# Moving six state updates of the first scan group, and starting two sets of weight sums in the pooling stage

## The chip, the cores and the metric

The kernel runs on one core of one Trainium2 chip. A core has a matrix engine (PE, with PEld for its weight loads), a vector engine (DVE), a scalar engine (ACT), GpSimd (POOL), and SyncE (SP), which here only issues transfers. POOL computes next to nothing in this kernel: it issues transfers too, those that add into memory among them. Each engine works through its own list of instructions in the order in which the program placed them; an instruction waits on semaphores for what it reads and for the buffer that it overwrites. All transfers share 16 DMA engines. The metric is the device time of one execution in microseconds (us).

## The reference

One decoder layer over 528 positions (16 learned ones ahead of 512) of width 1024, in float32. Cut to what matters here:

```python
u = rmsnorm(h, mix_norm_w);  proj = u @ w_in            # pool, z, x/B/C, dt, gates
y_pool = (pool_mixer(proj[pool]) * pool_scale) @ w_pool_up
# pool_mixer: causal means over 2, 4, 8, 16 positions minus the input, then 256x256 per group
xbc = silu(causal_depthwise_conv(proj[xBC], conv_w, conv_b))     # 4 taps
# scan: 8 groups of 4 heads, chunks of 128 positions
cb     = einsum("bclgn,bcsgn->bclsg", c, b)
y_diag = einsum("bclsg,bclsgr,bcsgrp->bclgrp", cb, exp(a_cs_l - a_cs_s) * mask, xdt)
states = einsum("bclgn,bclgr,bclgrp->bcgrpn", b, decay, xdt)
h_next = chunk_decay * h + state                        # over the chunks
y_off  = einsum("bclgn,bcgrpn,bclgr->bclgrp", c, h_prev, exp(a_cs))
y_ssd  = (rmsnorm_groups((y_diag + y_off + d_skip * x) * silu(z)) * norm_w) @ w_ssd_out
h = h + (gate_pool * y_pool + gate_ssd * y_ssd) @ w_o
v = rmsnorm(h, mlp_norm_w);  hid = relu(v @ w_ff1);  h = h + (hid * hid) @ w_ff2
out = rmsnorm(h, final_norm_w)[:, 16:]
```

## The kernel before

**Products.** Every float32 factor is split into a rounded part and a rest (`whi`, `wlo` for weights; `uh`, `ul` for the normed input), and a product is three matmuls: high by high, low by high, high by low. A weight block (128 x 1024, 512 KB) comes by an SP transfer into one of three `raw` buffers, ACT casts `whi` out of it (line 111 or 132) and DVE subtracts to get `wlo` (line 113 or 133). Many large products are made in Strassen's manner, from sums of blocks with one product less. Sums of weight blocks needed for that are made ahead by POOL transfers, from DRAM to DRAM, some of which add: `weight_steps` issues eight for a set of `f1` and four for a set of `f2`, into tensors that the profile calls `f_t` and `f_s`. An adding transfer waits until the copy below it has landed. SP loads the finished sums much later, as `t`, `s` or `rawf`.

**Stages.** Start and the projections of group 0, to about 75 us; the scan of groups 0 to 7, each woven with the projections and convolutions of the next group, to about 455; the pooling stage, to about 553; the merge of both branches under the gates; the output projection `wo`; then the two layers of the MLP, which run into each other from about 672 on.

**The scan step.** `ssd` takes a group through these steps: it masks and decays the chunk products (`abc`, line 679, "masked" in the code), updates the state over the chunks (`st`, a multiplication on line 675 and an addition on line 676 for each of three chunks), multiplies the states by C (`po`, line 688) and the masked products by x (`py`, line 694), and sums both in `yt`. Meanwhile the projections of the next group go through PE into PSUM (`px`) and through a convolution of one first tap and three further taps on DVE (line 442) into `bt`, `ct` and `xc`. Wide PSUM tiles come from two buffers, so the third `px` tile can only begin when DVE has read the last tap out of the first.

**The pooling stage.** `pool_pair` forms four products of one pool group out of two weight blocks a1 and a2 (`raw_block`, SP's line 126): `whiA`/`wloA` from a1, then `sm` (lines 985 and 987) and two more sums, `whiS`, `whiD`, `whiB` and their rests. The projected input `pu` is averaged by DVE (`pw`, line 962), split into `ph` and `pl` (lines 973 and 974) and multiplied by the group's matrix (`pg`, `pool_mix`). POOL loads the kept accumulators (`acc`) and gates (`m`, line 1090) meanwhile.

**After the merge.** POOL loads the residual `ht` in four parts (line 1202) as soon as the buffers of the normed input are free, and then issues what is left of the sets, because the loop behind it runs `while sets`. In the MLP, ACT applies relu (1391) and the square (1392), DVE makes the sums of Strassen's left factors (`r`, lines 1518 to 1521, and `vs`, lines 1440 to 1443) and their rests (1449, 1513, 1523), and adds finished products from PSUM (`alpha`) to `ht` or takes them away (line 1240). A product on PE that needs alpha's PSUM again waits for that line.

**What sets the order.** The program is written in the order of the stages, and a scheduler places the instructions on the engines by priority: `tc.high_priority(n)` gives an instruction a place n instructions sooner, `tc.issue_after(x)` puts it behind x in the order.

Of the kernel before, what the change touches and what calls it, by code (L numbers as in the profile page):

```python
# [12 lines left out]
ALU = mybir.AluOpType  # L13
# [39 lines left out]

SETS_AT = {0: 1, 1: 1, 2: 2, 3: 1, 4: 2, 5: 2, 6: 1, 7: 1}
PIECES = {4: 21, 7: 14}
SETS_POOL = 0

PLAIN = 4

# [5 lines left out]
def kernel(ctx: ExitStack, tc, xT, x, w, fx, f1, f2, vec, fnw, out):  # L65
    nc = tc.nc
    act, dve, pe, pool = nc.scalar, nc.vector, nc.tensor, nc.gpsimd
# [47 lines left out]
    def block(behind=None, cast_behind=None):  # L115
        t = block_tiles()
        with tc.high_priority(100):
            block_load(t, slice(0, 1024))
            block_split(t, slice(0, 1024), behind, cast_behind)
        return t[2:]  # L120
# [51 lines left out]
    cdec = const.tile([P, 4, HEADS], F32, name="cdec")  # L172
# [17 lines left out]
    gate_d = [dram.tile([P, SEQ], F32, name=f"gate_d{d}") for d in range(NK)]  # L190
# [157 lines left out]
    for t, name in ((rsh, "dgh"), (rsl, "dgl")):  # L348
        d = pre.tile([NT, 6, NT], F32R, tag="sq", name=name, bufs=2)
# [3 lines left out]
    for i in range(2):  # L353
        pb = psum1(f"pb1_{i}")
        c = slice(3 * i, 3 * i + 3)
# [235 lines left out]
    def bc(ap, n):  # L591
        return ap.unsqueeze(len(ap.shape)).to_broadcast(list(ap.shape) + [n])

    def ssd(g, cur):

        xc, bt, ct, zt = cur
        hs = slice(R * g, R * g + R)
        tok = lambda c: slice(NM + c * P, NM + (c + 1) * P)
        ctok = lambda c: slice(c * P, (c + 1) * P)
        flat = lambda t: t.rearrange("p r d -> p (r d)")  # L600
# [45 lines left out]
        def decay():  # L646
            act.activation(abc[:, :2], abc[:, :2], AF.Exp, scale=-1.0)
            return act.activation(abc[:, 2:], abc[:, 2:], AF.Exp)
# [14 lines left out]
        st = [gs.tile([P, R, 64], F32, tag=f"st{c}", name=f"st{c}_{g}") for c in range(4)]  # L663
        pss = [psum1(f"pst{g}_{b}") for b in range(2)]
        pv = [pss[c // 2][:, (c % 2) * 256 : (c % 2) * 256 + 256] for c in range(4)]
# [5 lines left out]
        if g == G - 1:  # L671
            with tc.issue_after(st0.ins):
                decay()
        for c in range(3):
            dve.tensor_tensor(st[c + 1], st[c], bc(cdec[:, c, hs], 64), op=ALU.mult)
            last_state[g] = dve.tensor_tensor(flat(st[c + 1]), flat(st[c + 1]), pv[c + 1], op=ALU.add)
        for rs_ in ((slice(0, 2), slice(2, R)) if g == G - 1 else (slice(0, R),)):
            n = rs_.stop - rs_.start
            masked[g] = dve.tensor_tensor(dm[:, rs_], dm[:, rs_], cbm.unsqueeze(1).to_broadcast([P, n, 4, P]),
                                          op=ALU.mult)  # L680
        mark[0] = st[3][:, 0, :1]
        yield

# [45 lines left out]
    late_cast, last_state = [None], {}  # L729
    done, abc_load, masked, y_first, squared, b_meta, x_decayed = {}, {}, {}, {}, {}, {}, {}  # L730
# [17 lines left out]
    m1 = {}  # L748
# [23 lines left out]
    def weight_steps():  # L772
        t = sets.pop(0)
        src = {"fx": fx, "f1": f1, "f2": f2}[t[0]][t[1]]
        o = {n: wsum[(*t, n)] for n in SUMS[t[0]]}
        put = nc.gpsimd.dma_start
        yield put(o["t1"], src[B11])
        yield put(o["s3"], src[B12])
        yield put(o["t1"], src[B12], accum_op=ALU.add)
        if "t2" in o:  # L780
            yield put(o["t2"], src[B22])
        yield put(o["s3"], src[B22], accum_op=ALU.add)
        if "t2" in o:
            yield put(o["t2"], o["t1"], accum_op=ALU.add)
            yield put(o["t4"], src[B21])
            yield put(o["t4"], o["t2"], accum_op=ALU.add)

    def weight_sums():
        for end in weight_steps():
            pass  # L790
        return end
# [142 lines left out]
    for g in range(G):  # L934
        nxt = group_tiles(g + 1) if g + 1 < G else None
        fill = [group_proj(g + 1, nxt, GATE_AT.get(g))] if nxt else [out_part()]
        if g == 4:
            fill = [out_half()] + fill
        weave(ssd(g, cur), fill, 2 if g == 4 else 1, weight_sums_at(SETS_AT[g], PIECES.get(g, 12)),
              [sums_of_u(g)] if g in SUMS_AT else [])  # L940
        cur = nxt
# [26 lines left out]
    def pooled_halves(t, s, copied=None):  # L968
        ph = gp.tile([P, SEQ], F32R, tag="ph", name=f"ph{t}", bufs=3)
        pl_ = gp.tile([P, SEQ], F32R, tag="pl", name=f"pl{t}", bufs=3)  # L970

        with tc.issue_after(copied.ins) if copied is not None else nullcontext():
            act.copy(ph, s[:, NM:])
        dve.tensor_tensor(pl_, s[:, NM:], ph.bitcast(F32), op=ALU.subtract)
        return ph, pl_
# [57 lines left out]
    def pool_mix(gi, pooled, wgb):  # L1033
        ps = [psum1(f"pg{gi}_{j}") for j in range(2)]
        wh, wl = wgb
        for j in range(2):
            os = [(gi % 2) * 512 + k * 256 + j * P for k in range(2)]
            mm3s(ps[j], [((wh[:, o : o + P], wl[:, o : o + P]), pooled[k]) for k, o in enumerate(os)])
        for j in range(2):
            t = 2 * gi + j  # L1040
            h = yp.tile([P, SEQ], F32R, tag="yh", name=f"yph{t}")
            l = yp.tile([P, SEQ], F32R, tag="yl", name=f"ypl{t}")
            mixed[:] = [act.activation(h, ps[j], AF.Copy, scale=col(V_PS, t)),
                        dve.scalar_tensor_tensor(l, ps[j], col(V_PS, t), h.bitcast(F32),
                                                 op0=ALU.mult, op1=ALU.subtract)]
            yps[t] = (h, l)

    def gate_ssd(d):
        ps = psum1(f"pgs{d}")
        proj(narrow(ps), block(), U)  # L1050
        gt = gtp.tile([P, SEQ], F32, tag="gt", name=f"gs{d}")
        act.activation(gt, ps, AF.Sigmoid, bias=col(V_BG, NK + d))
        return gt

    for d in range(NK):
        t_load = nc.gpsimd.dma_start(acc[d], acc_d[d])
    for _ in range(SETS_POOL):
        with tc.issue_after(t_load.ins):
            t_load = weight_sums()
    pend = [pooled_halves(*a) for a in pool_pair(POOL_ORDER[0])]  # L1060

    un = units()
# [11 lines left out]
    for n in range(1, 4):  # L1074
        pend, ahead = nxt, None
        if n < 3:
            nxt, ahead = pool_pair(POOL_ORDER[n + 1]), POOL_ORDER[n + 1]
        if n == 2:
            wgb = block()
        else:  # L1080
            gts.append(gate_ssd(MERGE[len(gts)]))

        pend = [pooled_halves(*a, copied.get(ahead)) for a in pend]
        with tc.issue_after(last[ahead].ins) if n < 3 else nullcontext():
            pool_mix(POOL_ORDER[n], pend, wgb)
        if n == 1:
            for d in MERGE:
                with tc.issue_after(mixed[0].ins):
                    if d < NK - 1:
                        nc.gpsimd.dma_start(m1[d], gate_d[d])  # L1090
    pool_stack.close()
    tf_stack.close()
    wo_stack = ExitStack()
# [548 lines left out]
    c = NC - 1  # L1642
# [14 lines left out]
    for t in range(4):  # L1657
        T, st = t // 2, slice((t % 2) * P, (t % 2 + 1) * P)
# [187 lines left out]
```

## Time and profile before

| | |
|---|---|
| median of 3 runs | 1000.0 us (999.92 to 1001.16) |
| profiled execution | 1001.71 us |
| span of its trace | 1000.0 us |
| PE busy | 987.8 us, 99% of the span |
| DVE busy | 803.9 us |
| ACT busy | 602.2 us |
| granted PE clock | 0.998 |
| POOL transfers | 67.51 MB, 26.4% of 16 DMA engines' span |
| SP transfers | 109.00 MB, 32.7% |

The span is 1.7 us shorter than the execution's time; what lies outside it is start and end. PE is idle for 12.2 us of the span. A row of a timeline has the start, the duration, the engine and line, the tiles written and read, the number of instructions merged, and in brackets the idle time ahead with what ended it. A DVE instruction's successor starts a little before its own written end, so the cost of one in a row is read from start to start.

### The profile page before, as it was taken

Reading aid. Unit: us, or ns where it says so; the run is one execution under the profiler, and the core shown is the slowest. Engines: PE = TensorE matmul, PEld = TensorE weight load, DVE = VectorE, ACT = ScalarE, POOL = GpSimd, SP = SyncE. Lnnn points to the kernel's source line nnn. Section 1 sums busy time; section 2 is a strip of 40 time slices with the busy share of each in tenths; the row PEclk is TensorE's granted clock in tenths of the full one; section 3 lists DMA queues with packets and bytes.
Section 4 is the critical chain, followed back from the end, with each engine's and each line's share of the span. In section 5 each row is a group of like instructions: output and inputs, shape, how many; then the busy total and the mean of one; then the engine's idle time right before and its main releaser. Section 6 shows DMA issues by size and latency. Waiting matters only on the chain.

```text
span 1000.0 us, 15672 instructions
## 1 busy us (share of the span) xinstructions
PE 987.8 (99%) x6035; PEld 873.8 (87%) x6035; DVE 803.9 (80%) x1162; ACT 602.2 (60%) x855; POOL 119.5 (12%) x215
## 2 busy tenths in 40 slices
PE   9999999999999999999999999999999999999997
PEld 7889998989889999978898888888789999999986
DVE  7978997879845888988789666975988888888885
ACT  7657839495924658574345433477666656656654
POOL 0011321211212212223200001121000000000000
PEclk9999999999999999999999999999999999999999
DMA  7284968666798848768723723899354454454332
GB/s 261 78 254 149 268 197 214 190 191 212 230 271 235 245 129 259 226 163 171 271 85 127 253 85 112 228 243 314 92 190 148 148 190 144 152 186 150 129 106 85
DMA packets 61803, 184.52 MB, mean 185 GB/s; under 512 B 7072, under 2 KB 8416, under 8 KB 60704
## 3 DMA queue, kind: packets, MB, share of 16 engines
q1 hardware_dynamic: 39456, 109.00, 32.7%
q0 software_dynamic: 18240, 67.51, 26.4%
q10 hardware_dynamic: 4032, 7.00, 1.9%
q8 instruction: 47, 0.77, 0.3%
q14 instruction: 28, 0.23, 0.1%
HBM read 173.13 MB, written 58.59 MB: 232 GB/s over the span
## 4 chain that ended last, share of the span: by engine, by line
PE 93%; ACT 3%; DVE 2%; DMA 1%; issue 0%; SPq 0%; ACTq 0%; DVEq 0%
PE px L1465 8%; PE px L215 8%; PE alpha L1533 6%; PE pz L215 6%; PE px L1468 4%; PE px L218 4%; PE alpha L1536 3%; PE pgp L215 3%; PE pz L218 3%; PE pgs L215 3%; PE py L694 2%; PE pqx L509 2%; PE pso L146 1%; PE pgp L218 1%; PE wo_alpha L1226 1%; PE po L688 1%
## 5 line engine op out<-in xcount | busy, mean ns | idle before, releaser
L113 DVE TENSOR_TENSOR wlo<-raw,whi 128x1024 fp32r<-128x1024 f32 (+2 forms) x88 | 102.0, 1171 | 46.8 <-ACT whi L111 31.0
L111 ACT CAST whi<-raw 128x1024 fp32r<-128x1024 f32 (+2 forms) x88 | 87.2, 1011 | 70.3 <-PE pso L147 15.3
L215 PE MATMUL px<-uh,whi 128*128 128x264 f32 (+1 forms) x320 | 80.9, 291 | 0.0
L218 PE MATMUL px<-ul,whi 128*128 128x264 f32 (+1 forms) x320 | 78.8, 285 | 0.0
L1240 DVE TENSOR_TENSOR ht<-ht,alpha 128x1024 f32<-128x1024 f32 x35 | 42.7, 1220 | 29.1 <-PE alpha L1533 29.1
L215 PEld LDWEIGHTS px<-uh,whi 128*128 128x128 f32 x320 | 60.4, 189 | 0.9 <-issue 0.7
L1162 ACT CAST shi<-rawf 128x1024 fp32r<-128x1024 f32 x42 | 44.2, 1053 | 28.0 <-PE alpha L1536 18.3
L218 PEld LDWEIGHTS px<-ul,whi 128*128 128x128 f32 x320 | 60.2, 188 | 0.4 <-issue 0.2
L1533 PE MATMUL alpha<-shi,hh 128*128 128x512 f32 x140 | 55.3, 395 | 2.0 <-DVE ht L1240 1.9
L1536 PE MATMUL alpha<-shi,hl 128*128 128x512 f32 x140 | 54.7, 391 | 0.0
L1163 DVE TENSOR_TENSOR slo<-rawf,shi 128x1024 fp32r<-128x1024 f32 x42 | 51.2, 1219 | 0.6 <-ACT shi L1162 0.6
L1468 PE MATMUL px<-vsl,shi 128*128 128x256 f32 x192 | 47.4, 280 | 0.0
L1465 PE MATMUL px<-vsh,shi 128*128 128x256 f32 x192 | 47.4, 281 | 0.0
L215 PE MATMUL pz<-uh,whi 128*128 128x512 f32 x112 | 43.7, 390 | 0.0
L218 PE MATMUL pz<-ul,whi 128*128 128x512 f32 x112 | 43.6, 389 | 0.0
L215 PE MATMUL px<-uh,wlo 128*128 128x264 f32 (+1 forms) x320 | 41.8, 283 | 0.0
L215 PEld LDWEIGHTS px<-uh,wlo 128*128 128x128 f32 x320 | 39.9, 188 | 0.0
L1533 PE MATMUL alpha<-slo,hh 128*128 128x512 f32 x140 | 37.4, 389 | 0.0
L1465 PEld LDWEIGHTS px<-vsh,shi 128*128 128x128 f32 x192 | 36.2, 188 | 0.9
L1468 PEld LDWEIGHTS px<-vsl,shi 128*128 128x128 f32 x192 | 36.1, 188 | 0.9
L1468 PE MATMUL px<-vl,shi 128*128 128x256 f32 x144 | 36.1, 283 | 0.0
L1465 PE MATMUL px<-vh,shi 128*128 128x256 f32 x144 | 36.0, 282 | 0.0
(599 smaller groups left out, 3064.8 us busy)
## 6 DMA issues: line engine op xcount, KB each, us to landing
raw<-in_w SPq DMA_DIRECT2D x96, 512.0 KB, 4.4
f_t<-in_f POOLq DMA_DIRECT2D x38, 512.0 KB, 7.4
f_s<-in_f POOLq DMA_DIRECT2D x26, 512.0 KB, 7.3
b<-in_f SPq DMA_DIRECT2D x21, 512.0 KB, 4.5
rawf<-in_f SPq DMA_DIRECT2D x36, 256.0 KB, 2.9
rawf<-f_t SPq DMA_DIRECT2D x36, 256.0 KB, 2.9
abc<-acs_d POOLq DMA_DIRECT2D x8, 1024.0 KB, 7.6
f_t<-f_t POOLq DMA_DIRECT2D x12, 512.0 KB, 6.7
```

The source lines that it names most:

```text
L111: act.copy(hi[:, c], raw[:, c])
L113: dve.tensor_tensor(lo[:, c], raw[:, c], hi[:, c].bitcast(F32), op=ALU.subtract)
L215: pe.matmul(o, wt, rhs[0][k][:, c], start=part == 0 and k == 0, stop=part == 1 and k == NK - 1)
L218: mm[0] = pe.matmul(o, wt, rhs[1][k][:, c], start=False, stop=False)
L509: at = pe.matmul(o, wk, f[k][0], start=start and not low and k == 0, stop=stop and low == 1 and k == 3, skip_group_check=True)
L1162: splits.append((act.copy(hi, src), dve.tensor_tensor(lo, src, hi.bitcast(F32), op=ALU.subtract)))
L1163: dve.tensor_tensor(lo, src, hi.bitcast(F32), op=ALU.subtract)))
L1240: added[0] = dve.tensor_tensor(o, o, src, op=op)
L1465: pe.matmul(ps, m, f[k][0], start=start and not low and k == 0, stop=stop and low == 1 and k == 3, skip_group_check=True)
L1468: pe.matmul(ps, m, f[k][1], start=False, stop=False, skip_group_check=True)
L1533: pe.matmul(ps[t], hh[:, p, seg, st], m, start=bool(first and not low and p == 0), stop=bool(last and low and p == 1), skip_group_check=True)
L1536: pe.matmul(ps[t], hl[:, p, seg, st], m, start=False, stop=False, skip_group_check=True)
```

## The change

The change has two parts.

**In `ssd`.** The six instructions that update the states were issued ahead of the masking, without a priority. In group 0 they are now issued behind it, with a place 100 instructions sooner. In the other groups the code's order is as before.

On DVE, in group 0, behind the masking. `abc` is the masked product, `st1_0`, `st2_0`, `st3_0` are the states of the three chunks, `px1_17` and `px1_25` the projections that the convolutions into `bt1` and `ct1` read. Before:

```order
L679 TENSOR_TENSOR abc0_931<-abc0_931,cbm0_1054 128x2048
L442 SCALAR_TENSOR_TENSOR bt1_928<-px1_17_987,vs_82,bt1_928 128x527
L675 TENSOR_TENSOR st1_0_1057<-st0_0_1056,cdec_87 128x256
L442 SCALAR_TENSOR_TENSOR bt1_928<-px1_17_987,vs_82,bt1_928 128x526
L676 TENSOR_TENSOR st1_0_1057<-st1_0_1057,pst0_0_1060 128x256
L442 SCALAR_TENSOR_TENSOR bt1_928<-px1_17_987,vs_82,bt1_928 128x525
L675 TENSOR_TENSOR st2_0_1058<-st1_0_1057,cdec_87 128x256
L442 SCALAR_TENSOR_TENSOR ct1_929<-px1_25_1074,vs_82,ct1_929 128x512
L676 TENSOR_TENSOR st2_0_1058<-st2_0_1058,pst0_1_1061 128x256
```

And now, on the same engine at the same place:

```order
L683 TENSOR_TENSOR abc0_931<-abc0_931,cbm0_1054 128x2048
L676 TENSOR_TENSOR st1_0_1057<-st0_0_1056,cdec_87 128x256
L442 SCALAR_TENSOR_TENSOR bt1_928<-px1_17_987,vs_82,bt1_928 128x527
L677 TENSOR_TENSOR st1_0_1057<-st1_0_1057,pst0_0_1060 128x256
L442 SCALAR_TENSOR_TENSOR bt1_928<-px1_17_987,vs_82,bt1_928 128x526
L676 TENSOR_TENSOR st2_0_1058<-st1_0_1057,cdec_87 128x256
L442 SCALAR_TENSOR_TENSOR bt1_928<-px1_17_987,vs_82,bt1_928 128x525
L677 TENSOR_TENSOR st2_0_1058<-st2_0_1058,pst0_1_1061 128x256
L442 SCALAR_TENSOR_TENSOR ct1_929<-px1_25_1074,vs_82,ct1_929 128x512
```

Each state instruction moved ahead of one tap of a convolution: between the masking and the addition of `st1_0` there is one tap now and not two, and between the masking and the last tap of `bt1` there are three state instructions and not two.

On PE, at the same place: `po` multiplies the states, `px_2` is the next projection, whose first four rows stand for the whole. One piece of the difference:

```order
-L688 MATMUL po_1_1217<-ct_518,st_0_1056 128x128
-L688 MATMUL po_1_1217<-ct_518,st_0_1057 128x128
+L695 MATMUL po_0_1137<-ct_518,st_0_1056 128x128
+L701 MATMUL py_0_1142<-abc_931,xdt_933 64x128 x8
+L695 MATMUL po_0_1137<-ct_518,st_0_1057 128x128
+L695 MATMUL po_1_1217<-ct_518,st_0_1056 128x128
+L695 MATMUL po_1_1217<-ct_518,st_0_1057 128x128
 L215 MATMUL px_2_1157<-uh_94,whi_1159 128x264
 L218 MATMUL px_2_1157<-ul_102,whi_1159 128x264
 L215 MATMUL px_2_1157<-uh_94,whi_1159 128x264
 L218 MATMUL px_2_1157<-ul_102,whi_1159 128x264
+L695 MATMUL po_0_1137<-ct_518,st_0_1058 128x128
```

The products of the states ahead of `px_2` are the same as before; the one of the second chunk's state (`st_0_1058`) stands 8 matmuls earlier within `px_2`, and that of the third likewise.

**In the pooling stage.** `SETS_POOL` is 2 instead of 0, and its loop stands behind the last load of `m` instead of behind those of `acc`. So two sets of sums, one of `f1` and one of `f2`, are issued there, and the loop behind `ht` has two sets left instead of four. On POOL, from the last load of `m` on, before (`f_t_504` to `f_t_507` are the first set, `f_t_508` and `f_s_509` the second, `f_t_510` begins the third):

```order
L1090 DMA m_3_5001<-gate_d_138 128x512
L1202 DMA ht<-in_x 128x1024 x4
L777 DMA f_t_504<-in_f 128x1024
L778 DMA f_s_505<-in_f 128x1024
L781 DMA f_t_506<-in_f 128x1024
L779 DMA f_t_504<-in_f 128x1024
```

And now, on the same engine:

```order
L785 DMA f_s_509<-in_f 128x1024
L786 DMA f_t_508<-in_f 128x1024
L789 DMA f_s_509<-in_f 128x1024
L1209 DMA ht<-in_x 128x1024 x4
L784 DMA f_t_510<-in_f 128x1024
L785 DMA f_s_511<-in_f 128x1024
```

Twelve transfers of two sets stand between `m` and `ht`, and the third and fourth set follow `ht` at once.

```diff
-SETS_POOL = 0
+SETS_POOL = 2
...
-        for c in range(3):
-            dve.tensor_tensor(st[c + 1], st[c], bc(cdec[:, c, hs], 64), op=ALU.mult)
-            last_state[g] = dve.tensor_tensor(flat(st[c + 1]), flat(st[c + 1]), pv[c + 1], op=ALU.add)
+        def states():
+            for c in range(3):
+                dve.tensor_tensor(st[c + 1], st[c], bc(cdec[:, c, hs], 64), op=ALU.mult)
+                last_state[g] = dve.tensor_tensor(flat(st[c + 1]), flat(st[c + 1]), pv[c + 1], op=ALU.add)
+
+        if g:
+            states()
...
             masked[g] = dve.tensor_tensor(dm[:, rs_], dm[:, rs_], cbm.unsqueeze(1).to_broadcast([P, n, 4, P]),
                                           op=ALU.mult)
+        if not g:
+            with tc.issue_after(masked[g].ins), tc.high_priority(100):
+                states()
...
-    for _ in range(SETS_POOL):
-        with tc.issue_after(t_load.ins):
-            t_load = weight_sums()
     pend = [pooled_halves(*a) for a in pool_pair(POOL_ORDER[0])]
...
                     if d < NK - 1:
-                        nc.gpsimd.dma_start(m1[d], gate_d[d])
+                        t_load = nc.gpsimd.dma_start(m1[d], gate_d[d])
+            for _ in range(SETS_POOL):
+                with tc.issue_after(t_load.ins):
+                    t_load = weight_sums()
```

## The prediction

> **What bounds the kernel now.** I read the page first: busy time of the engines, then the chain that ended last.
>
> ```profile
> PE 987.8 (99%) x6035; PEld 873.8 (87%) x6035; DVE 803.9 (80%) x1162; ACT 602.2 (60%) x855; POOL 119.5 (12%) x215
> ...
> PE 93%; ACT 3%; DVE 2%; DMA 1%; issue 0%; SPq 0%; ACTq 0%; DVEq 0%
> ...
> L1533 PE MATMUL alpha<-shi,hh 128*128 128x512 f32 x140 | 55.3, 395 | 2.0 <-DVE ht L1240 1.9
> ```
>
> PE is busy 99% of 1000.0 us, so the change can only win a part of the 12.2 us in which PE is idle, and only by ending a wait of PE. It removes no matmul. Conversely it loses whatever new wait it gives PE. So the whole question is which PE waits stand near the two edited places, and I read the timelines there. Two waits are in reach: one ahead of `po` in group 0, and the one ahead of `alpha` that the third row sums up.
>
> **Part one, the state updates of group 0.** The timelines of DVE and of PE there:
>
> ```profile
> 86.39 0.76 DVE L442 SCALAR_TENSOR_TENSOR bt<-px,vs,bt 128x527 f32<-128x527 f32 x1
> 87.07 0.42 DVE L675 TENSOR_TENSOR st<-st,cdec 128x256 f32<-128x256 f32 x1
> 87.40 0.76 DVE L442 SCALAR_TENSOR_TENSOR bt<-px,vs,bt 128x526 f32<-128x526 f32 x1
> 88.08 0.41 DVE L676 TENSOR_TENSOR st<-st,pst 128x256 f32<-128x256 f32 x1
> 88.40 0.76 DVE L442 SCALAR_TENSOR_TENSOR bt<-px,vs,bt 128x525 f32<-128x525 f32 x1
> ...
> 90.07 0.41 DVE L676 TENSOR_TENSOR st<-st,pst 128x256 f32<-128x256 f32 x1
> ```
> ```profile
> 88.54 0.94 PE L688 MATMUL po<-ct,st 128*128 128x128 f32 x6 [0.85 <-DVE st L676]
> 89.23 0.38 PE L215 MATMUL px<-uh,whi 128*128 128x264 f32 x1
> ...
> 90.80 0.38 PE L688 MATMUL po<-ct,st 128*128 128x128 f32 x2
> ```
>
> PE waits 0.85 us at 88.54 for the state's addition, which ends at 88.08 + 0.41 = 88.49. From start to start a tap costs 0.68 us (86.39 to 87.07, 87.40 to 88.08) and a state instruction 0.33 (87.07 to 87.40). In the new order one tap less stands ahead of that addition: it starts at 86.39 + 0.33 + 0.68 = 87.40 and ends at 87.81, so `po` can go on at about 87.87, that is 0.68 sooner. But `px` behind it, which starts at 89.23, needs the PSUM buffer that the third tap of `bt` reads last. Now that tap ends at 88.40 + 0.76 = 89.16, just ahead of 89.23, so the wait costs nothing extra. In the new order three state instructions stand ahead of it instead of two, and it ends at 89.16 + 0.33 = 89.49. PE does its six `po` matmuls from 87.87 to 88.56 (0.69, as from 88.54 to 89.23), then waits for the tap and begins `px` at about 89.55, 0.3 later than before. The stall is not removed, it moves one step on and grows by one state instruction. **Part one: +0.3 us.** From below it is bounded by the case that the tap doesn't hold `px` up (-0.7), from above by the added instruction (+0.35).
>
> What else moved here is covered. The third tap now starts at 88.40 + 0.33 = 88.73, and the second state's addition 0.68 behind it, at 89.41, to end at 89.82 (before: 90.07 + 0.41 = 90.48). The `po` that needs it stood at 90.80 and now stands behind four `px` matmuls instead of twelve, which began at 89.55, so near 90.05. The taps of `ct` and the weight rest behind them come up to 0.7 later; the tiles that they free are needed by the projection after this one, several microseconds on. In the other groups only the neighbourhood in group 1 shifts, and there is no PE wait to win or, by the same count, to make. On POOL the next `abc` load falls behind one more sum, at 0.5 to 0.8 us each, long before it is used.
>
> **Part two, what the moved sums give.** What POOL does around `ht`, before:
>
> ```profile
> 486.41 1.75 POOL L1090 DMA_DIRECT2D m<-gate_d  x3 [0.37 <-DMA raw<-in_w]
> ...
> 619.06 1.58 POOL L1202 DMA_DIRECT2D ht<-in_x  x3 [130.90 <-PE pgs L215]
> ...
> 621.37 0.53 POOL L777 DMA_DIRECT2D f_t<-in_f  x1
> ...
> 656.75 0.83 POOL L777 DMA_DIRECT2D f_t<-in_f  x1
> ...
> 697.79 0.82 POOL L782 DMA_DIRECT2D f_s<-in_f  x1 [0.76 <-DMA f_s<-in_f]
> ```
>
> POOL's queue has nothing to do for 130.90 us. Two sets took it from 621.37 to 656.75, 35 us, the next two from there to 697.79 and some landing time. Started at 488.2, the first two end near 488 + 35 = 523 or a little later, ninety microseconds ahead of `ht`: `ht` isn't delayed, it waits for PE as before. The last two then start at 621.4 and are issued by about 665. Between 665 and 706 the queue is empty where it was full. What stood in that stretch:
>
> ```profile
> raw<-in_w SPq DMA_DIRECT2D x5, 512.0 KB, 9.7
> ...
> 680.00:690.00 10.00, 10.00 (x45) 8.26 (x44) 2.45 (x2) 5.96 (x9) 1.87 (x3) 1.00 1.04 334
> ...
> 686.24 1.05 ACT L111 CAST whi<-raw 128x1024 fp32r<-128x1024 f32 x1 [4.04 <-DMA raw<-in_w]
> ...
> 687.33 1.23 DVE L113 TENSOR_TENSOR wlo<-raw,whi 128x1024 fp32r<-128x1024 f32 x1 [5.40 <-ACT whi L111]
> ...
> 710.00:720.00 10.00, 10.00 (x46) 8.29 (x45) 10.00 (x18) 5.11 (x7) 0.00 (x0) 1.00 0.17 52
> ...
> 724.01 1.22 DVE L1240 TENSOR_TENSOR ht<-ht,alpha 128x1024 f32<-128x1024 f32 x1
> ...
> 722.41 1.07 PE L149 MATMUL pf<-vh,wlo 128*128 128x512 f32 x4
> 725.37 0.47 PE L1533 MATMUL alpha<-shi,hh 128*128 128x512 f32 x1 [1.89 <-DVE ht L1240]
> ...
> 730.15 0.50 PE L1533 MATMUL alpha<-shi,hh 128*128 128x512 f32 x1
> ```
>
> (The columns of the stretch rows are PE, PEld, DVE, ACT and POOL busy, the granted clock, the DMA engines' share, GB/s.) Read from the top: from 660 to 690 five weight loads had a median of 9.7 us from issue to landing; the DMA engines were full, 1.04 in the last ten microseconds. ACT idles 4.04 us for such a load and casts at 686.24, DVE idles 5.40 behind it, and is busy 2.45 us in ten. It never catches up: from 710 to 720 it is busy 10.00 of 10, and it comes to line 1240 at 724.01. PE, which had no wait until then, stops for 1.89 us ahead of `alpha`. With the loads at 3.4 to 4 us (the rows below), ACT and DVE get up to 4 us back at 686, of which 1.9 and what follows are needed. **Gain: -2.3 us**: the 1.89, the slower restart (0.47 instead of 0.39) and about 0.3 at the next `alpha`, at 730.15, which starts late in the same way. Bounds: 0, if DVE is late there for another reason, and -2.3, since PE has no other wait between 660 and 730.
>
> **Part two, what the moved sums cost.** They now run from 488 to 523 or 529 beside the pooling stage's loads:
>
> ```profile
> 480.00:490.00 10.00, 9.74 (x59) 8.63 (x59) 8.08 (x13) 3.94 (x6) 3.74 (x7) 1.00 1.04 376
> ...
> 510.00:520.00 10.00, 10.00 (x85) 10.00 (x84) 9.69 (x15) 4.67 (x9) 0.00 (x0) 1.00 0.12 47
> 520.00:530.00 10.00, 10.00 (x62) 8.96 (x61) 10.00 (x17) 3.42 (x7) 0.00 (x0) 1.00 0.48 157
> ...
> 491.55 15.97 SPq L126 DMA_DIRECT2D raw<-in_w  x3
> ...
> 520.39 1.54 SPq L126 DMA_DIRECT2D raw<-in_w  x2
> ...
> raw<-in_w SPq DMA_DIRECT2D x1, 512.0 KB, 3.4
> ...
> raw<-in_w SPq DMA_DIRECT2D x1, 512.0 KB, 3.5
> ...
> raw<-in_w SPq DMA_DIRECT2D x1, 512.0 KB, 7.4
> ...
> 511.76 0.69 DVE L985 TENSOR_TENSOR sm<-raw,raw 128x512 f32<-128x512 f32 x1
> ...
> 519.14 1.22 DVE L133 TENSOR_TENSOR wloD<-raw,whiD 128x1024 fp32r<-128x1024 f32 x1
> ...
> 520.65 0.65 PE L1004 MATMUL pxx<-t0h,wloD 128*128 128x264 f32 x4
> ...
> 524.00 1.06 ACT L132 CAST whiA<-raw 128x1024 fp32r<-128x1024 f32 x1 [3.25 <-DVE pu L1026]
> ...
> 528.66 0.68 DVE L974 TENSOR_TENSOR pl<-pu,ph 128x512 fp32r<-128x512 f32 x1
> ...
> 530.17 0.39 PE L147 MATMUL pg<-pl,whi 128*128 128x512 f32 x1
> ```
>
> The first two rows are SP's issues: the last of the three ends at 507.5 and was issued at 507.19, the first of the two at 520.39. Their times to landing are 3.4 and 3.5; the 7.4 is a load between 615 and 660, beside the four parts of `ht` and the first sums. With the DMA engines nearly idle (0.12) a load is fast. These two have little room, since DVE is busy 9.7 to 10 of 10 and hands lateness on. The load of 507.19 lands at 510.6 and is used at 511.76; `wloD`, further on in DVE's unbroken work, ends at 520.36 and PE needs it at 520.65. Room: 1.2 + 0.3 = 1.5. The load of 520.39 lands at 523.9, and ACT casts at 524.00, with no room; `wloA` follows at once, `pl` ends at 529.34 and PE takes it at 530.17. Room: 0.83. So with every load longer by d, PE loses about (d - 1.5) + (d - 0.83), each where it is positive.
>
> For d there are two ends: 0, and 7.4 - 3.4 = 4.0 beside far more traffic than here. I take an estimate between them: at 376 GB/s (the stretch that is full) 512 KB move in 1.4 us; if a load shares the engines with one other queue by turns, these 1.4 double, d = 1.4, a load of 4.8. Then PE loses 0 + 0.57. The next loads are issued when DVE releases a buffer, so the lateness goes on into them; I put **+1.0 us**, and 0 and 5.7 (2.5 + 3.2 at d = 4) as ends. It is nearer to 0 because the adding transfers wait for each other and leave one or two in flight, not five.
>
> [...]
>
> **The sum.** +0.3 - 2.3 + 1.0 = -1.0 us. The profiled execution took 1001.71 with a span of 1000.0; the same difference against the median of 1000.0 gives 999.0.
>
> **Rivals.** (a) *The pooling stage becomes the place that waits.* The loads there take 7 us, PE waits ahead of `wloD` and `pg`: d = 4, +0.3 - 2.3 + 5.7 = +3.7, 1003.7. For it: DVE has no idle time there to give. Against: 35 us of POOL's transfers carry two sets, so the engines aren't full all the time. It decides from (d - 1.5) + (d - 0.83) = 2.0 on, d = 2.2, a load of 5.6 us.
> (b) *The loads are hidden.* d stays below 0.8, PE loses nothing there: +0.3 - 2.3 = -2.0, 998.0, and 997.0 if the third tap doesn't hold `px` up either. For it: POOL's sums pause whenever an adding transfer waits for the copy below it (0.76 us ahead of the one at 697.79), and a load that falls into a pause is as fast as alone. Against: the median of 9.7 us in the stretch that was full.
> (c) *The wait at 725 stays.* DVE's full stretch from 700 on is work, not lateness: then +0.3 + 1.0 = +1.3, 1001.3. For it: 10.00 of 10 with no gap in which to catch up. Against: the 7.6 us idle in the ten ahead of 690 are all ahead of that work.
> That the sums don't get to the early place at all is excluded by POOL's order; only the idle 130.90 us stand between.
>
> **How the numbers follow.** The forecast has 0.47, with its own range from 998.1 to 1000.5 (d from 0.8 to 2.2). Rival (a) has 0.16, (b) 0.24, (c) 0.13. Three runs of before spread over 1.24 us, so 0.2%, 2.0 us, is about what can be told from no change. Faster than 998.0 are most of (b) and the lower edge of the forecast: 0.27. Slower than 1002.0 are nearly all of (a) and a little of (c): 0.17. The rest, 0.56, lies within. The range goes from 997.0, the end of (b), to 1002.2, past (c) and into (a).
>
> **What the profile after would show.** For part one: `po` goes on near 87.9 and a PE wait of about 1.0 ahead of `px`, put down to DVE's `bt`. For the gain: weight loads of 3.4 to 5 us between 665 and 690, no 4.04 at ACT's cast, line 1240 ahead of 722.4, no wait ahead of `alpha`. For the cost: POOL busy at 488 to 525, loads of 4 to 5 us there, and PE waits of half a microsecond near 530. I'm wrong if PE waits add up to more than 2 us between 505 and 545, if the 1.89 is still there, or if the wait at 88.54 goes without another in its place.

## The result and the profile after

The changed kernel is slower: a median of 1004.58 us (999.56 to 1007.63, 20 runs) against 1000.52 (999.27 to 1002.82, 20 runs), a ratio of 1.0036 with a 95% interval of 1.0023 to 1.0048. The forecast was 999.0 in a range up to 1002.2. Rival (a), the pooling stage as the place that waits, is nearest.

The profiled execution took 1003.91 us with a span of 1002.2, 2.2 more than before's span. The two medians lie 4.1 us apart, or 3.6 by the ratio; the traces account for 2.2 of it, and what the rest is stays open. Busy times hardly differ; what differs is where PE waits. The view of PE's waits, after:

```profile
PE pg L147 <- DVE pl L981: 2.2, 2, 1.2
...
PE psp L146 <- ACT sp L878: 1.5, 1, 1.5
PE pz L1011 <- ACT pu L1027: 0.8, 1, 0.8
PE px L215 <- DVE bt L442: 0.7, 1, 0.7
PE po L695 <- DVE st L677: 0.2, 1, 0.2
```

And before:

```profile
PE alpha L1533 <- DVE ht L1240: 1.9, 1, 1.9
...
PE po L688 <- DVE st L676: 0.9, 1, 0.9
PE pz L1004 <- ACT pu L1020: 0.3, 1, 0.3
```

The wait ahead of `alpha` is gone, as forecast. The one ahead of `po` became one ahead of `px`, as forecast. New are 2.2 us ahead of `pg`, in the pooling stage, and 0.5 more ahead of `pz` near 481.

Comparing the start of the same matmul in both traces gives where the 2.2 us came from. Up to 86 us the changed kernel is 0.35 ahead (start-up, ahead of the change). It loses 0.37 near 88, wins 0.57 near 131, loses 0.57 near 481, loses 4.43 between 529.5 and 533, and wins 2.28 at 723 and 730. The sum is 2.2.

The 4.43 in the timelines of the changed kernel, ACT's and DVE's rows first, then PE's, then three stretches with PE's clock (the columns are as in the prediction):

```profile
527.55 1.05 ACT L132 CAST whiA<-raw 128x1024 fp32r<-128x1024 f32 x1 [6.76 <-DMA raw<-in_w]
...
528.63 1.23 DVE L133 TENSOR_TENSOR wloA<-raw,whiA 128x1024 fp32r<-128x1024 f32 x1 [3.40 <-ACT whiA L132]
...
532.18 0.68 DVE L981 TENSOR_TENSOR pl<-pu,ph 128x512 fp32r<-128x512 f32 x1
```
```profile
529.52 0.42 PE L146 MATMUL pg<-ph,whi 128*128 128x512 f32 x1
531.11 0.50 PE L147 MATMUL pg<-pl,whi 128*128 128x512 f32 x1 [1.17 <-DVE pl L981]
531.45 0.40 PE L146 MATMUL pg<-ph,whi 128*128 128x512 f32 x1
532.92 0.79 PE L147 MATMUL pg<-pl,whi 128*128 128x512 f32 x1 [1.07 <-DVE pl L981]
...
536.67 0.28 PE L1011 MATMUL pxx<-uh,whiA 128*128 128x264 f32 x1
```
```profile
531.00:532.00 1.00, 0.73 (x2) 0.30 (x2) 1.00 (x3) 0.00 (x0) 0.00 (x0) 1.00 0.00 0
...
534.00:535.00 1.00, 1.00 (x4) 0.81 (x3) 1.00 (x3) 0.40 (x1) 0.00 (x0) 0.50 0.00 0
...
537.00:538.00 1.00, 1.00 (x10) 1.00 (x9) 1.00 (x2) 0.56 (x1) 0.00 (x0) 1.00 0.00 0
```

This is the chain that the forecast priced, only longer. ACT waits 6.76 us for the load issued at 520.41 and casts at 527.55 instead of 524.00. DVE's `wloA` follows at 528.63 instead of 525.11, `pl` ends at 532.86 instead of 529.34, and PE, which was there at 529.7, loses 1.36 and 1.37 us ahead of two matmuls. Behind these waits comes something that was in no term: the granted clock is 0.50 from about 532.9 to 536.3, for 3.4 us. Nine matmuls take from 532.92 to 536.67, 3.75 us, where they take 0.227 each, 2.04, at full clock: 1.71 us more. 2.73 of waiting and 1.71 of slow clock are, up to rounding, the 4.43.

The load itself, and POOL's queue beside it:

```profile
raw<-in_w SPq DMA_DIRECT2D x1, 512.0 KB, 7.0
```
```profile
487.87 0.54 POOL L784 DMA_DIRECT2D f_t<-in_f  x1
...
517.34 0.84 POOL L786 DMA_DIRECT2D f_t<-in_f  x1 [5.49 <-DMA f_t<-in_f]
518.63 0.82 POOL L789 DMA_DIRECT2D f_s<-in_f  x1 [0.45 <-DMA f_s<-in_f]
623.52 0.57 POOL L1209 DMA_DIRECT2D ht<-in_x  x1 [104.07 <-PE pgs L215]
...
659.79 0.82 POOL L789 DMA_DIRECT2D f_s<-in_f  x1 [1.67 <-DMA f_s<-in_f]
```

It took 7.0 us instead of 3.5, beside the second set's two adding transfers issued at 517.34 and 518.63. The gain's side is as forecast: POOL's last issue is at 659.79 instead of 697.79, the five weight loads from 664 to 690 have a median of 5.0 us instead of 9.7, line 1247 (before 1240) comes at 725.43, ahead of `alpha` at 727.78, and `alpha` begins without a wait:

```profile
raw<-in_w SPq DMA_DIRECT2D x5, 512.0 KB, 5.0
```
```profile
725.43 1.22 DVE L1247 TENSOR_TENSOR ht<-ht,alpha 128x1024 f32<-128x1024 f32 x1
```
```profile
726.87 1.07 PE L149 MATMUL pf<-vh,wlo 128*128 128x512 f32 x4
727.78 0.39 PE L1540 MATMUL alpha<-shi,hh 128*128 128x512 f32 x1
```

PE comes there 4.46 us later than before, which is more than the wait of 1.89, so this trace alone doesn't show that DVE became early enough. The traces of experiments 3 and 7 do: PE comes there 0.5 and 0.2 us later than before, and doesn't wait either.

The runs of the changed kernel spread more than those of before. Four of the 20 took 999.6 to 1000.6 us, the other 16 took 1003.7 to 1007.6. The mean granted clock of those four was 0.999 to 1.0, of the others 0.995 to 0.999. The traced one, 1003.91, is among the 16. So the times of four executions in 20 show no loss; none of the four was traced, so why is not shown, nor what the slowest lost.

### The profile page after: what moved, and what is told of

The parts are those of the page before. It is cut to its first block, busy times and chain, and to the rows that moved or that the text cites. A ratio compares the mean times of both kernels' runs of the same rounds, so it can differ in the third digit from the quotient of the medians.

```text
span 1002.2 us, 15676 instructions
## 1 busy us (share of the span) xinstructions
PE 989.2 (99%) x6035; PEld 875.2 (87%) x6035; DVE 804.2 (80%) x1162; ACT 602.6 (60%) x855; POOL 122.3 (12%) x215
## 3 DMA queue, kind: packets, MB, share of 16 engines
q1 hardware_dynamic: 39456, 109.00, 33.1%
q0 software_dynamic: 18240, 67.51, 26.3%
## 4 chain that ended last, share of the span: by engine, by line
PE 92%; ACT 3%; DVE 2%; DMA 2%; issue 0%; ACTq 0%; DVEq 0%
PE px L1472 8%; PE px L215 8%; PE alpha L1540 6%; PE pz L215 6%; PE px L1475 4%; PE px L218 4%; PE alpha L1543 3%; PE pgp L215 3%; PE pz L218 3%; PE pgs L215 3%; DMA raw<-in_w 2%; PE pqx L509 2%; PE py L701 2%; PE pso L146 1%; PE pgp L218 1%; PE wo_alpha L1233 1%
```

## The experiments

Theory L: the second set's transfers slow the loads of the pooling stage, PE waits for what hangs on them, and its clock falls behind the wait. Ratios are against the kernel before, with 95% intervals.

**1. The state updates alone, and 2. the sums alone.**

```diff
-SETS_POOL = 2
+SETS_POOL = 0
```

> The new place of the state updates alone, no sums moved. Theory L (the sums slow the pooling stage's loads, and PE's clock falls behind the wait): the whole loss hangs on the sums, so this kernel is within 1 us of the kernel before, with the wait of 1.9 us ahead of alpha still there, +0.4 us near 88 us, -0.6 us near 131 us, and the latter lost again near 481 us. Rival S (the state updates' new place costs the time): 2 to 4 us slower than before.

1001.24 us, ratio 1.0005 (0.9995 to 1.0014): no difference. On every engine but POOL its trace has the order of the changed kernel, so nothing but the place of POOL's transfers separates the two. The changes near 88, 131 and 481 us came as expected. The wait of 1.9 us did not stay whole:

```profile
PE alpha L1540 <- DVE ht L1247: 1.0, 1, 1.0
```

PE comes there 2.34 us late in this trace, 1.57 of them lost behind a fall of the clock near 446 us, which the last section shows, and leaves it 1.41 late. A wait that still stands gives back a part of what was lost ahead of it, so there are probably not 1.89 us to be won in every execution of before.

For the sums alone `ssd` is as before and `SETS_POOL` is 2:

> The two sets of sums in the pooling stage alone, the states as before. Theory L: the same as the changed kernel, 3 to 5 us above before, waits of 2 to 3 us ahead of pg near 530 us and a granted clock near 0.5 just behind them. Rival S: 2 us faster than before, since the wait ahead of alpha goes and nothing else comes.

1006.23 us, ratio 1.0057 (1.0041 to 1.0073). That is more than the 3 to 5 us expected. The loss belongs to the sums; rival S falls. In its trace, of the slowest of the six runs (1009.79), the load of this place took 8.1 us, and PE waits 0.5 us or more ahead of five matmuls of the stage:

```profile
PE pg L147 <- DVE pl L974: 2.2, 2, 1.2
...
PE pg L146 <- ACT ph L973: 1.0, 1, 1.0
...
PE pxx L1004 <- ACT pu L1017: 0.9, 1, 0.9
...
PE pxx L1004 <- ACT pu L1011: 0.5, 1, 0.5
```

That the sums alone lose more than with the states moved isn't settled: the two intervals overlap.

**3. One set instead of two, with the states moved, and 4. without.**

```diff
-SETS_POOL = 2
+SETS_POOL = 1
```

> One set in the pooling stage instead of two; it ends near 515 us, ahead of the loads issued at 520.4 to 523.7. Theory L: those loads take 3.5 to 4.5 us again, no wait ahead of pg above 0.3 us, clock 1.0 there; the sums behind ht end near 690 us instead of 665, so a part of the wait ahead of alpha may stay: -0.5 to -2.3 us against before. Rival D (DVE is too full in the pooling stage whatever the loads do): the wait ahead of pg stays above 1 us.

> One set in the pooling stage, the states as before. Theory L: the wait ahead of alpha goes as with the states moved: 0.5 to 2.3 us faster than before. If the states' new place matters beside the sums, this differs from the run with one set and moved states by more than 1 us.

1000.05 us, ratio 0.9991 (0.9982 to 0.9999), and 1000.08, ratio 0.9990 (0.9978 to 1.0002). The load of 520.9 beside no transfer of POOL's, with ACT's cast behind it and the products that had waited, in the run with the states moved:

```profile
raw<-in_w SPq DMA_DIRECT2D x1, 512.0 KB, 3.6
```
```profile
524.55 1.05 ACT L132 CAST whiA<-raw 128x1024 fp32r<-128x1024 f32 x1 [3.30 <-DVE pu L1033]
```
```profile
530.22 0.39 PE L147 MATMUL pg<-pl,whi 128*128 128x512 f32 x1
530.45 0.39 PE L146 MATMUL pg<-ph,whi 128*128 128x512 f32 x1
530.67 0.39 PE L147 MATMUL pg<-pl,whi 128*128 128x512 f32 x1
```

No wait: rival D falls. The second set, whose transfers meet the loads of 520 to 524, makes the whole loss with the states moved. The first set meets loads too: those of about 492 and 493 take 5.7 and 5.8 us instead of 3.5 and 4.4, and PE doesn't wait, because they have 4 us of room or more.

With the states as before, the first set alone does cost something. In that trace the stage runs about 2.3 us later, and the load that the prediction gave 1.5 us of room, issued at 509.50 here, meets an adding transfer of the first set. DVE waits for the load, and PE behind DVE and ACT:

```profile
raw<-in_w SPq DMA_DIRECT2D x1, 512.0 KB, 6.1
```
```profile
515.63 0.69 DVE L985 TENSOR_TENSOR sm<-raw,raw 128x512 f32<-128x512 f32 x1 [1.48 <-DMA raw<-in_w]
```
```profile
PE pxx L1004 <- ACT pu L1017: 0.7, 1, 0.7
```

PE loses 1.4 us there, where the prediction's first term, d - 1.5 with the load's 6.11 - 3.35 as d, gives 1.3. In the trace of the sums alone the same load took 7.0; the term gives 2.2, and PE lost 2.4. Both kernels have the order of before on every engine but POOL. So which loads a set meets differs from trace to trace, and the first set isn't free either; whether the place of the states or the execution decides it is not shown.

One set less behind `ht` is also enough for the wait ahead of `alpha`: it is gone in both traces.

**5. and 6. PE kept busy ahead of `pg`.** Twelve, then six matmuls are added, into a tile that the real product overwrites:

```diff
             os = [(gi % 2) * 512 + k * 256 + j * P for k in range(2)]
+            if gi == 2 and j == 0:
+                for _ in range(12):
+                    pe.matmul(ps[0], wh[:, os[0] : os[0] + P], pooled[0][0], start=True, stop=True)
```

> The changed kernel with 12 extra matmuls of 0.23 us ahead of the first pg product of the second pool group, into a PSUM tile that the real product overwrites: PE works through the 2.7 us in which it waited. Theory L with the clock as a part of its own: the waits ahead of pg fall below 0.5 us, the granted clock stays at 1.0, and the time falls by 1.5 to 2.5 us against the changed kernel, to 1002 to 1003. Rival C (the clock falls for another reason, such as the transfers or the power of the whole stretch): the clock still falls and the time stays at 1004 to 1005.

> The changed kernel with 6 extra matmuls of 0.23 us ahead of the first pg product of the second pool group, half of those of the filled kernel. PE's idle time ahead of pg falls to about 1.4 us, less than the 1.9 us ahead of alpha in before, behind which the clock stayed at 1.0. If the clock's fall is a part of the loss by itself: clock at 1.0 there and 1.5 us less than the changed kernel. If DVE's lateness would have stopped PE anyway (as in the filled kernel): clock at 1.0, but waits of 1 us or more come up behind pg, and the time is that of the changed kernel or more.

1006.44 us, ratio 1.0056 (1.0043 to 1.0068), and 1005.37, ratio 1.0051 (1.0039 to 1.0064). With six, PE's waits and the clock there:

```profile
PE pxx L1011 <- ACT pu L1018: 1.2, 1, 1.2
PE pg L147 <- DVE pl L981: 1.1, 1, 1.1
```
```profile
534.00:536.00 2.00, 2.00 (x10) 1.62 (x10) 2.00 (x4) 0.00 (x0) 0.00 (x0) 1.00 0.00 0
```

The clock stays at 1.0 there in both traces, with the transfers beside the loads as before. The ten runs of these two kernels have mean clocks of 0.998 to 1.0, where 11 of the 20 of the changed kernel have 0.997 or less. That speaks for a fall that hangs on PE's idle time, and against rival C; two traces don't prove it, since the wait of 1.4 to 1.5 us near 443 us was followed by a fall in five traces and by none in six (last section). But the time doesn't come back, against the 1002 to 1003 expected with twelve: between 481 and 553 these kernels lost 5.7 us (six) and 6.6 (twelve) where the changed kernel lost 4.4, with new waits of 1.2 to 1.5 ahead of `pxx`, the second of the outcomes named for six. That fits DVE's and ACT's lateness stopping PE a little later when its clock doesn't fall. It isn't a clean test: with the added matmuls the scheduler places a few instructions of ACT and DVE in another order behind `pg`, so that on ACT the casts `whiD` and `whiB` now stand ahead of the `pu` that PE waits for, and the load took 7.6 and 7.8 us instead of 7.0. So whether the 1.71 us can be had by themselves stays open.

**7. Both sets held back to the merge, 8. to the mixing of the second pool group, 9. to the merge without the states.** A one-column copy on POOL waits for a tile; the sums stand behind it, and the loop in the pooling stage goes. The added lines of the first:

```diff
         dve.tensor_tensor(acc[d], acc[d], m1[d], op=ALU.add)
+        if n == 1:
+            t_load = pool.tensor_copy(seen, acc[d][:, :1])
+            for _ in range(SETS_POOL):
+                with tc.issue_after(t_load.ins):
+                    t_load = weight_sums()
```

> The changed kernel, but POOL holds the two sets until the second accumulator of the merge is written, near 571 us: a one-column copy on POOL, which reads that accumulator, stands ahead of them. From there to 606 us only single loads with room run. Theory L: the pooling stage is as before (no wait ahead of pg, loads of 520 at 3.5 us, clock 1.0), the wait ahead of alpha is gone: 2 us faster than before, 998 to 999. Rival D (DVE is too full in the pooling stage whatever the loads do): the wait ahead of pg stays and the time is within 1 us of the changed kernel.

> The two sets held to the merge as in the held run, the states as in the kernel before. If the gain of the held run is the wait ahead of alpha alone, this is as fast: 1 to 2.3 us faster than before. If the states' new place gives or costs something that lasts, it differs from the held run by more than 0.5 us; the trace should show the wait of 0.85 us near 88 us and, near 481 us, PE as late or as early as in before.

999.77 us, ratio 0.9989 (0.9980 to 0.9998), and 999.81, ratio 0.9988 (0.9979 to 0.9997). Both beat both kernels; the 2 us expected of the first were not reached. POOL with the states moved:

```profile
572.51 0.44 POOL L1198 COPY seen<-acc 128x1 f32<-128x1 f32 x1 [85.33 <-DVE acc L1196]
572.89 0.54 POOL L784 DMA_DIRECT2D f_t<-in_f  x1
...
604.27 0.82 POOL L789 DMA_DIRECT2D f_s<-in_f  x1 [0.16 <-issue]
619.24 2.16 POOL L1211 DMA_DIRECT2D ht<-in_x  x4 [14.15 <-PE pgs L215]
```

The sums run from 572.9 to about 610 beside single loads, nothing waits ahead of `pg` or `alpha`, and the span is 997.9, 2.1 less than before. The ratios give 1.1 and 1.2 us, with 0.2 to 2.1 as the interval, so the gain of 2.3 that the trace shows is above what the runs show. The states' place makes no difference that these runs resolve. One expectation failed: without the states moved PE waits 1.30 us near 481, the longest of all traces there, and not as in before.

The hold to the mixing reads a tile of the second group's mix instead, near 531 us:

> As the run before, but held only until the second pool group is mixed, near 531 us, so that the two sets run from 532 to 567 us beside the 16 loads at the start of the merge. The order on every other engine is that of the changed kernel. Theory L says the waits ahead of pg are gone, since the loads of 520.4 to 523.7 have landed by then; what the 16 loads lose shows whether the merge has room: 998 to 999 if they have 4 us each, above 1001 if not. Rival D: the wait ahead of pg stays.

1001.69 us, ratio 1.0005 (0.9993 to 1.0017). The loads from 538 to 574, held to the mixing first, and then held to the merge, where the sums start behind them:

```profile
raw<-in_w SPq DMA_DIRECT2D x11, 512.0 KB, 8.1
wob<-in_w SPq DMA_DIRECT2D x6, 512.0 KB, 10.8
```
```profile
raw<-in_w SPq DMA_DIRECT2D x11, 512.0 KB, 4.1
wob<-in_w SPq DMA_DIRECT2D x6, 512.0 KB, 5.6
```

Ahead of the second pool group's `pg` nothing waits now. Seventeen loads took about twice as long, and PE lost 1.5 us by it, at `pg` near 551. In the changed kernel one load without room that took twice as long cost 4.4, the fall of the clock included. The order on every engine but POOL is the same in the changed kernel and in this one, so it is the place of the transfers alone that counts, and in it the room of the loads beside them.

## Why the prediction was wrong

**What bounds, and that only PE's waits count: right.** Every part of the difference is a PE wait that came or went, but for the clock.

**Part one, +0.3: right at its place, and without effect on the whole.** `po` went on at 87.56 in a trace that is 0.35 us ahead at this point (forecast: 87.87), and `px` waits 0.75 us for `bt`: the wait moved one step on, in all seven traces with the states moved. The loss there is 0.37. What I ruled out, a change in group 1, happened: 0.57 us were won near 131, where `po` and `py` now alternate less often with `px`. PE then came to 481 earlier and waited there as much longer for ACT's `pu` in this trace. That wait isn't tied to the states: it is under 0.2 us in two traces with the states moved, and 1.30 in one without. The states alone measure 1.0005: nothing that the runs resolve.

**The gain, -2.3: right in the trace** (2.28), for the stated reason, and larger than the 1.1 and 1.2 us by which the runs of the held kernels, which don't pay the price, are faster.

**The cost, +1.0: wrong, and this is the step that failed.** It measured 4.43: 2.73 of waiting and 1.71 of clock. The places, the two rooms and the chain were right; the room at `pg` of 0.83 predicts the wait well once d is known: 7.0 - 3.5 = 3.5, less 0.83, is 2.67, and 2.73 were lost. Mis-sized was d, put at 1.4 and measured as 3.5. I halved the bandwidth of a load by turns of equal size, which was my assumption and which no run shows, and then argued that the true d is nearer to 0. What the runs show in its place is the 3.5, and that a packet of POOL's queue took longer than one of SP's. From the page of before, and the row of SP's queue from 480 to 530:

```profile
q1 hardware_dynamic: 39456, 109.00, 32.7%
q0 software_dynamic: 18240, 67.51, 26.4%
```
```profile
q1 hardware_dynamic: 1373, 4.97, 27.6%
```

32.7% of 16 engines' 1000 us, over 39456 packets, is 0.133 us for a packet of SP's; 26.4% over 18240 is 0.232 for one of POOL's. A load of 512 KB at 3.6 KB per packet (4.97 MB in 1373) is 145 packets. An estimate with as many packets of POOL's as the load has gives 145 x 0.232 us over 16 engines, 2.1 us. How many go by beside a load, no row that I had shows; in the changed kernel it was 244 of POOL's beside 289 of SP's (below). With d = 2.1 the wait would be (2.1 - 1.5) + (2.1 - 0.83) = 1.9, which takes away nearly all of the gain. Measured were d of 2.8 and 2.0 for the loads of 491.6 and 492.7, 0.5 and 0.8 for those of 507.2 and 508.2, and 3.5, 2.7 and 2.0 for the three from 520.4 on. So one d for both loads was wrong too. From issue to landing POOL's queue had 64.0 and 64.3% of the engines' time beside the first two, 14.1 and 29.3% beside the next two, and 64.5, 45.8 and 18.3% beside the last three: a share of 64% went with a d of 2.0 to 3.5, though the last load lost 2.0 at 18.3%. The estimate is still low for the load that decides. While that one ran, from 520.41 to 527.45, the queues of the changed kernel had these rows:

```profile
q0 software_dynamic: 244, 0.87, 64.5%
q1 hardware_dynamic: 289, 1.07, 37.7%
```

64.5% of 16 engines' 7.04 us, over 244 packets, is 0.298 us for a packet of POOL's, all of them of the two adding transfers; SP's took 0.147. At 0.298 the same estimate, 145 packets over 16 engines, gives 2.7 of the 3.5 us. The rest fits the packets of SP's next load, of which about 100 more went by than beside the same load in before (289 packets against 189): 6 on an engine, at 0.147 us each. That it is these is not shown. Nor were 9.7 and 7.4 us the marks of "far more traffic": one set in flight was enough for 7.0.

**The clock: missing.** A wait was priced at its length. 1.71 us of the 4.43 are slow matmuls behind it. The prediction had no term for it. Nothing in the trace of before showed a clock below 1.0 while PE had matmuls; its longest wait of PE, 1.89 us ahead of `alpha`, left it at 1.0.

**The rivals.** (a) had the mechanism, the place and d (4.0 against 3.5), and its 1003.7 is the nearest number. That nearness is partly luck: 2.5 of its 5.7 us stood for a wait at `wloD` that the changed kernel's trace doesn't have, and the 1.71 of clock were not in it. I gave it 0.16, against the only row of a load beside POOL's sums that I had quoted, the 7.4. (b) falls with d. (c) falls: the wait of 725 went, with two sets moved and with one.

## What to carry over

A transfer moved into an idle queue isn't free because the queue is idle: here a load beside two such transfers took 7.0 us instead of 3.5. Look up which loads run at its new hour and what room each has until its first use, and put the transfers where the room is. Held back by 85 us, the same twelve transfers turned +3.6 us into -1.1, by the ratios. Price a load beside another queue by a measured one where there is one: here equal shares gave d = 1.4, equal numbers of packets 2.1, both estimates, and the trace 3.5. And reckon with slower matmuls behind a wait of PE: here they cost 1.71 us behind 2.73 of waiting.

## What the runs showed of the hardware

In these traces PE's clock halved behind waits shorter than one that left it alone. In the changed kernel two waits of 1.36 and 1.37 us with two matmuls between them were followed by a clock of 0.50 for 3.4 us; in before a single wait of 1.89 us ahead of `alpha` was followed by none.

Nearly the same wait was followed by a fall in some executions and not in others. Every kernel here has a wait of 1.4 to 1.5 us ahead of `psp` near 443 us. The clock fell behind it in five of the eleven profiled executions, for 3.4 us each, and that cost 1.5 to 1.6 us. Without a fall (before), and with one (the states alone):

```profile
446.00:447.00 1.00, 1.00 (x11) 0.83 (x8) 1.00 (x3) 0.39 (x1) 0.11 (x1) 1.00 0.86 156
```
```profile
446.00:447.00 1.00, 1.00 (x12) 0.97 (x8) 1.00 (x3) 0.60 (x1) 0.32 (x1) 0.50 0.97 80
```

This is larger than most of what these experiments had to tell apart. It is likely a part of the spread between runs of one kernel: of 27 runs of before in one round (999.1 to 1005.2 us), the seven slowest have mean clocks of 0.996 to 0.998, the others but one 0.998 to 1.0. What makes the clock fall in one execution and not in another is not shown.
